# Last block pair: units in another order, the causal mask added by TensorE, and the squares for the value ranges spread over two pairs

## The chip, the cores and the metric

The kernel runs on one core of a Trainium2 chip, in one launch. TensorE (PE in the profile) multiplies matrices into PSUM, VectorE (DVE), ScalarE (ACT) and GpSimd (POOL) work on elements, and SyncE (SP) issues most of the transfers. The metric is the device time of one execution, in microseconds (us); less is better.

## The reference

One layer over 1024 rows of width 1024, in fp32. The input is normalised, scaled and shifted by terms that come from a conditioning vector, and projected to queries, keys, values and gates of two groups of eight heads of 64. One group is forgetting attention (softmax with an added term from a cumulative sum of log gates), the other stick-breaking attention. Each group's output is gated by SiLU, both are projected together, added to the input with a per-column gate, and normalised again:

```python
# forgetting attention, one block i of 128 queries against keys 0 .. 128 (i + 1)
s = einsum('bhqd,bhkd->bhqk', q, k) * HEAD_DIM ** -0.5
s = s + (f_q[..., :, None] - f_k[..., None, :])
s = where(k_pos[None, :] <= q_pos[:, None], s, -inf)
o = einsum('bhqk,bhkd->bhqd', softmax(s), v)
...
y = concat([y_fox * silu(fg), y_sb * silu(sg)]) @ w_out
x = layer_norm(ALPHA * x + gate * y) * ln_g + ln_b
```

## The kernel before

**Pairs and units.** The 16 heads are worked on as eight pairs `p` (0 to 3 stick-breaking, 4 to 7 forgetting). A unit is `(p, h, i)`: head `h` of a pair and query block `i` of 128 rows, against `i + 1` blocks of 128 keys. `order(p)` (lines 1228 to 1237) lists the 16 units of a pair; the main loop (line 1304) counts units as `k` from 0 to 127, and the last pair begins at `LAST` = 112. In the last pair the order is 7, 6 for head 0, 7, 6 for head 1, then 5, 4 twice, 3, 2 twice, 1, 0 twice.

**One unit of a forgetting pair.** `att_scores` (line 593) has PE write the scores into PSUM: two fp32r matmuls for each half of the keys (lines 606 and 607; there is one half up to 512 keys, else two). DVE adds the row `fb` of forget terms and takes the row's minimum (line 614), ACT takes the exponential with its sum (620), DVE the reciprocal (621, 622), ACT writes the high fp16 part (626) and DVE, one unit later, the low part (630). `cross` sends both through a transposing DMA on SP (567). The causal mask stands in `fb` itself: `att_causal` adds a 128x128 triangle of -1e30 to the diagonal block of the next unit's `fb` on DVE (591), in place, which works while the blocks of a head come in falling order. Five units later (`LAG_CROSSED`), when both blocks of a block pair `j` are there, `att_pv` multiplies by the values (701) and `att_sum` combines, gates and, for pairs before the last, queues a store to `y_dr` in DRAM (727, 728, 733; `send`, line 579). For the last pair the result stays on chip as `y7h` and `y7l` (738, 739). `LAST_HOMES` (538) gives each block pair of the last pair its place for the transposed parts.

**Fillers.** Between the units, PE's projection work is issued in small steps from one generator chain (`fillers`, line 1200): `gen_m(p, m)` projects q, k and the gates of pair `p`, `gen_v(g)` the values of two pairs. `FILL` says how many steps each pair takes. `beside(main, *sides)` issues one step of each side with each step of the main chain and runs the sides out at its end. The sides of the first group are `gen_gate` and `gen_ranges`. `gen_ranges` (378) loads the 12 raw value weights through the two `raw` buffers that the other weights use as well, squares and sums each on DVE (393), and three steps (`NORM_SPACE`) later comes to the next; at the end it derives a scale for each group of values, first used by `gen_v(1)`. `gen_forget` (475) is a side of a later group: it sums the log gates, and 16 steps (`FROW`) on has POOL write a triangle of ones `tri` into an `att` buffer (499, 500), which PE multiplies at once (504).

**Last pair.** Its fillers are `gen_last_g(7)` (1184): the gates, with `split_wo` beside each step, which splits one 128-row piece of the output weights into high (ACT, 1063) and low parts (half on DVE, half on POOL, 1064). The two gate accumulators use both PSUM buffers of tag `acc` and are emptied by ACT (320) and DVE (321).

**Output.** Rows come in eight tiles `t` of 128, in `OUT_ORDER`. `load_y(t)` (1077) loads the stored results of pairs 0 to 6 in two pieces and splits them on POOL (1084, 1085). `o_step` (1093) is three matmuls into an `acc` buffer (1104 to 1106), 16 such steps a tile; `o_half` (1110) applies the gate and adds the input on DVE (1123, 1124), takes statistics (1125), normalises (1132, 1136) and stores. From unit `LAST + OUT0` on, `TAIL` steps of output are issued after each unit, so the first tiles are worked on while the last pair's attention is still going; a tile's last step needs `y7h` and `y7l` of its rows.

**What sets the order.** PE's instructions stand in the order of the program (`manual_schedule`). The order on the other engines and in SP's queue is set by the framework's planner, from the same program, before the kernel runs; `after(...)` adds single constraints. Every engine and SP's queue then work through their lists in order.

Of the kernel before, what the change touches and what calls it, by code (L numbers as in the profile page):

```python
# [15 lines left out]
P = 128  # L16
SEQ = 1024
D = 1024
NB = 8
NPAIR = 8  # L20
# [11 lines left out]
def tile_hybrid_layer(  # L32
# [17 lines left out]
    nc = tc.nc  # L50
# [47 lines left out]
    GATE = 20  # L98
    NORM_SPACE = 3

# [277 lines left out]
    def gen_ranges():  # L378


        nc.gpsimd.tensor_copy(modc[:, 1, :], bss_sb[:, 1, :])
        m2 = rng[:, 0:2]
# [92 lines left out]
    def gen_forget():  # L475
# [13 lines left out]
        with after(*lows[-1:]):  # L489
# [4 lines left out]
                                     op0=ALU.add, op1=ALU.mult)  # L494
        for _ in range(FROW):
            yield
# [3 lines left out]
        nc.gpsimd.affine_select(out=tri, in_=tri, pattern=[[1, P]], base=0,  # L500
                                channel_multiplier=-1, compare_op=ALU.is_ge, fill=0.0)
        f_ps = s_tile("f_ps", 2)
        fp = f_ps[:, 0, :64]
# [33 lines left out]
    HOMES = ((1, 12), (2, 0), (1, 0), (0, 0))  # L537
    LAST_HOMES = ((1, 12), (4, 8), (2, 0), (4, 0), (1, 0), (0, 0), (0, 0), (4, 0))

# [53 lines left out]
    def att_scores(u, following):  # L593
# [10 lines left out]
        for s in halves:  # L604
            ks = slice(s * w, s * w + w)
            nc.tensor.matmul(S[:, s, :w], qst[p][h][:, qs], kst[p][h][:, ks], start=True, stop=False)  # L606
            nc.tensor.matmul(S[:, s, :w], z, klo[p][:, ks], start=False, stop=True)  # L607
        v3 = lambda a: a[:, :ke].rearrange("p (a b) -> p a b", a=ns)
        if p >= 4:
# [7 lines left out]
            pay(reduced)  # L617
            if following:
                att_causal(following)
# [467 lines left out]
    o_acc = {}  # L1087
    OUT_ORDER = (6, 7, 4, 5, 2, 3, 0, 1)

# [94 lines left out]
    def gen_last_g(p):  # L1184
# [14 lines left out]

    fillers = chain([  # L1200
        beside(chain([gen_rest(), gen_v(0, v0_w, range(4, NB)), gen_m(1, 2)]), gen_gate(), gen_ranges()),
        gen_m(2, 0), gen_m(2, 1), gen_v(1),
        beside(chain([gen_m(2, 2), gen_m(3, 0), gen_m(3, 1), gen_m(3, 2)]), gen_forget()),
# [9 lines left out]
    W0 = 100.0  # L1213
    OUT0 = 4
    TAIL = (2, 2, 2, 2, 2, 2, 4, 4, 4, 4, 8)
# [3 lines left out]
    LNLOAD = 7  # L1219
    YLOAD = (6, 9, 12, 14, 16)  # L1220
    done = [0]
# [6 lines left out]
    def order(p):  # L1228
        if p == 0:
            return [(p, h, i + d) for i in (0, 4) for h in range(2) for d in range(4)]  # L1230
        if p < FIRST_CROSSED:
            return [(p, h, i) for h in range(2) for i in range(NB)]
        if p < 4:
            return [(p, h, i + d) for h in range(2) for i in (6, 4, 2, 0) for d in range(2)]
        if p < NPAIR - 1:
            return [(p, h, i) for h in range(2) for i in reversed(range(NB))]
        return [(p, h, i + d) for i in reversed(range(0, NB, 2)) for h in range(2) for d in (1, 0)]

# [18 lines left out]
    LAST = 16 * (NPAIR - 1)  # L1257
    tail = chain([gen_out_first(6), gen_out_last(6)] + [gen_out(t) for t in OUT_ORDER[1:]])
    fill(4)
# [44 lines left out]
    for k in range(len(units) + LAG_CROSSED):  # L1304
        if k < 16 * 4:
            weights_turn(k)
            scores_turn(k)
        else:
            scores_turn(k)
            fill(want[2 * k + LEAD + 1])  # L1310
            weights_turn(k)
        send(k)
        fill(want[2 * k + LEAD + 2])
        if k >= LAST + OUT0:
            for _ in range(TAIL[min(k - LAST - OUT0, len(TAIL) - 1)]):
                next(tail, None)
        if k == LAST:
            load_y(6)
        if k == LAST + LNLOAD:
            load_ln()  # L1320
        for i, d in enumerate(YLOAD):
            if k == LAST + d:
                load_y(OUT_ORDER[i + 1])
# [64 lines left out]
```

## Time and profile before

| | |
|---|---|
| median of 3 runs | 670.23 us (669.97 to 673.47) |
| the profiled execution: its own time | 674.67 us |
| its span on the profile | 673.0 us |
| mean granted clock of TensorE | 0.976 |
| DMA, moved | 96.25 MB, mean 143 GB/s |
| all before the last pair, on the profile | 0 to 527 us |
| last pair and output, on the profile | 527 to 673 us |

All durations below are those of the profiled execution; the runs give the time. A row of a group reads: line of the kernel, engine, operation, output and input tiles, shapes, count, busy time, mean of one in ns, idle time of the engine ahead of it and who ended it. In the view of waits a row names who waited, for whom, the sum, the count and the longest. In a timeline row stand start, duration, engine, line, operation, tiles, shape, count and, in brackets, the idle time ahead and its releaser.

### The profile page before, as it was taken

How to read it: one execution, taken by the hardware profiler on the slowest of the kernel's cores; microseconds unless marked ns; L12 is line 12 of the kernel's file. 1: busy time of each engine (PE TensorE's matmuls, PEld its weight loads, DVE VectorE, ACT ScalarE, POOL GpSimd, SP SyncE). 2: the span in 40 equal slices, each digit the busy share in tenths (PEclk: the TensorE clock that was granted, in tenths of full speed). 3: DMA queues.
4: the chain of work that ended last, by engine and by line, in shares of the span. 5: the costliest groups of instructions: out<-in, count | busy, mean ns of one | idle time of the engine just before them, and what ended most of it. 6: DMA issues, size and time to landing. Idle time of an engine off the chain costs nothing. (4 is left out here: it accounts for less than half of the span.)

```text
span 673.0 us, 10856 instructions
## 1 busy us (share of the span) xinstructions
PE 634.2 (94%) x3526; PEld 532.4 (79%) x3526; DVE 518.8 (77%) x1027; ACT 398.2 (59%) x833; POOL 342.4 (51%) x429
## 2 busy tenths in 40 slices
PE   8999987999999989999999999999999859899995
PEld 4788876788899868788998888899888647688884
DVE  6787788986857887977967685876779698886756
ACT  5577354775657767677867675766659767421000
POOL 5660164965635685778566333331642376356412
PEclk9999998999999989999999999999999879799998
DMA  9983454211201164847466575865496899673301
GB/s 321 401 302 141 148 137 139 72 41 40 65 16 36 42 148 79 157 111 162 121 172 156 144 165 123 169 138 112 130 207 139 231 231 253 133 200 122 122 31 63
DMA packets 153800, 96.25 MB, mean 143 GB/s; under 512 B 118224, under 2 KB 133136, under 8 KB 153744
## 3 DMA queue, kind: packets, MB, share of 16 engines
q1 hardware_dynamic: 152160, 91.09, 53.1%
q10 hardware_dynamic: 1584, 4.47, 1.9%
q8 instruction: 28, 0.46, 0.3%
q14 instruction: 28, 0.23, 0.1%
HBM read 55.13 MB, written 7.90 MB: 94 GB/s over the span
## 5 line engine op out<-in xcount | busy, mean ns | idle before, releaser
L328 PE MATMUL m<-uh,whi 128*128 128x512 f32 x304 | 123.1, 405 | 1.6 <-DVE kl L315 1.6
L330 PE MATMUL m<-uh,wlo 128*128 128x512 f32 x304 | 120.2, 395 | 0.0
L329 PE MATMUL m<-ul,whi 128*128 128x512 f32 x304 | 120.1, 395 | 0.0
L652 POOL TENSOR_TENSOR be<-be,kp 128x127 f32<-128x127 f32 (+3 forms) x64 | 89.4, 1397 | 44.3 <-DVE kp L650 24.4
L733 POOL TENSOR_TENSOR ty<-ty,sg 64x256 f32<-64x256 f32 x64 | 47.4, 740 | 102.4 <-DVE ty L728 58.0
L646 DVE TENSOR_TENSOR_SCAN kp<-kp,floor 128x128 f32<-128x128 f32 (+3 forms) x64 | 58.5, 914 | 17.2 <-ACT kp L638 16.6
L606 PE MATMUL S<-k,q 128*128 128x512 f32 (+5 forms) x192 | 68.7, 359 | 2.1 <-DMA k<-k 2.1
L620 ACT ACTIVATE a<-a,nm 128x1024 f32<-128x1024 f32 (+3 forms) x64 | 49.7, 776 | 33.0 <-DVE nm L614 32.1
L330 PEld LDWEIGHTS m<-uh,wlo 128*128 128x128 f32 x304 | 57.4, 189 | 13.7
L328 PEld LDWEIGHTS m<-uh,whi 128*128 128x128 f32 x304 | 57.5, 189 | 12.8 <-issue 1.4
L630 DVE SCALAR_TENSOR_TENSOR home<-a,l,home 128x1024 f16<-128x1024 f32 (+3 forms) x64 | 62.7, 979 | 4.4 <-ACT home L626 3.2
L607 PE MATMUL S<-kl,qz 128*128 128x512 f32 (+5 forms) x192 | 65.9, 345 | 0.0
L329 PEld LDWEIGHTS m<-ul,whi 128*128 128x128 f32 x304 | 57.5, 189 | 9.8
L614 DVE CUSTOM_DVE_ANT_0 a<-S,fb 128x1024 f32<-128x1024 f32 (+3 forms) x64 | 48.1, 752 | 21.6 <-PE S L607 21.2
L626 ACT ACTIVATE home<-a,l 128x1024 f16<-128x1024 f32 (+3 forms) x64 | 49.2, 773 | 22.7 <-DVE l L622 11.7
L638 ACT ACTIVATE kp<-S 128x384 f32<-128x384 f32 (+4 forms) x96 | 43.7, 491 | 26.9 <-PE S L607 26.2
L701 PE MATMUL pv<-home,v_g 128*128 128x256 f16 x480 | 57.7, 269 | 1.3 <-DVE ty L728 0.7
L1104 PE MATMUL o<-woh,whi_y 128*128 128x512 f32 (+1 forms) x119 | 47.9, 403 | 11.1 <-POOL wol L1064 8.2
L701 PEld LDWEIGHTS <-v_g 128*128 128x128 f16 x480 | 44.3, 100 | 17.5 <-issue 11.8
L438 PE MATMUL v<-whi_v,uh 128*128 128x256 f32 (+1 forms) x192 | 54.7, 285 | 0.0
L440 PE MATMUL v<-wlo_v,uh 128*128 128x256 f32 (+1 forms) x192 | 54.4, 283 | 0.0
L439 PE MATMUL v<-whi_v,ul 128*128 128x256 f32 (+1 forms) x192 | 54.1, 282 | 0.0
(325 smaller groups left out, 1606.6 us busy)
## 6 DMA issues: line engine op xcount, KB each, us to landing
raw<-in_w_qkg_dram SPq DMA_DIRECT2D x38, 256.0 KB, 2.7
wss<-in_w_ss_dram SPq DMA_DIRECT2D x14, 512.0 KB, 8.4
x<-in_x_dram SPq DMA_DIRECT2D x8, 512.0 KB, 7.1
k<-k SPq DMA_DIRECT2D x32, 128.0 KB, 2.3
wg<-in_w_gate_dram SPq DMA_DIRECT2D x8, 512.0 KB, 4.9
fb<-f_dr ACTq DMA_DIRECT2D x8, 512.0 KB, 4.2
wor<-in_w_out_dram SPq DMA_DIRECT2D x8, 512.0 KB, 4.0
xr<-in_x_dram SPq DMA_DIRECT2D x8, 512.0 KB, 4.0
```

Source lines behind the costliest of these rows:

```text
L328: nc.tensor.matmul(acc, hi[:, c], u_hi[kt][:, s], start=(kt == 0), stop=False)
L329: nc.tensor.matmul(acc, hi[:, c], u_lo[kt][:, s], start=False, stop=False)
L330: nc.tensor.matmul(acc, lo[:, c], u_hi[kt][:, s], start=False, stop=(kt == NB - 1))
L438: nc.tensor.matmul(acc[:, :n], u_hi[kt][:, ts_], hi[:, s], start=(kt == 0), stop=False)
L439: nc.tensor.matmul(acc[:, :n], u_lo[kt][:, ts_], hi[:, s], start=False, stop=False)
L440: nc.tensor.matmul(acc[:, :n], u_hi[kt][:, ts_], lo[:, s], start=False, stop=(kt == NB - 1))
L606: nc.tensor.matmul(S[:, s, :w], qst[p][h][:, qs], kst[p][h][:, ks], start=True, stop=False)
L607: nc.tensor.matmul(S[:, s, :w], z, klo[p][:, ks], start=False, stop=True)
L630: lows[:] = [nc.vector.scalar_tensor_tensor(lo, ab, l, hi, op0=ALU.mult, op1=ALU.subtract)]
L646: last_dve = nc.vector.tensor_tensor_scan(rv, rv, floor[:, :ke - lo], initial=0.0, op0=ALU.mult, op1=ALU.max)
L652: nc.gpsimd.tensor_tensor(be[:, :ke - 1], be[:, :ke - 1], kp[:, 1:ke], op=ALU.mult)
L701: nc.tensor.matmul(acc[:, q0:256], vt[p][:, kb, h * P:(h + 1) * P], pt[:, 2 * kb + x_, q0:], start=(kb == 0 and x_ == 0), stop=(kb == last ...
```

## The change

The last pair's units come in the order 2, 3 for head 0, 2, 3 for head 1, then 0, 1 twice, 4, 5 twice and 6, 7 twice, and the output tiles in the order 2, 3, 0, 1, 4, 5, 6, 7; `LAST_HOMES` follows that order. As blocks no longer come in falling order, the mask of the last pair isn't added to `fb`: a third matmul, identity times triangle in fp32, adds it to the last 128 columns of the scores in PSUM, and `att_causal` is left out for the last pair. Output begins one unit later (`OUT0` 5), the first `load_y` stands at `LAST + 4` in place of `LAST`, the second at `LAST + 7` in place of `LAST + 6`.

`gen_ranges` waits for 18 steps before its first square and leaves five steps between squares; `gen_m(2, 0)` and `gen_m(2, 1)` move into the main chain that it runs beside. In `gen_forget`, `tri` is written eight steps earlier; the matmul that reads it stays where it was.

```diff
--- before.py
+++ after.py
@@ -96,7 +96,8 @@
     FLOG = 8
     FROW = 16
     GATE = 20
-    NORM_SPACE = 3
+    NORM_SPACE = 5
+    NORM_AT = 18
 
     def after(*instructions):
         stack = ExitStack()
@@ -378,6 +379,8 @@
     def gen_ranges():
 
 
+        for _ in range(NORM_AT):
+            yield
         nc.gpsimd.tensor_copy(modc[:, 1, :], bss_sb[:, 1, :])
         m2 = rng[:, 0:2]
         nc.vector.tensor_reduce(out=m2, in_=modc.rearrange("p k i -> p i k"), op=ALU.max,
@@ -492,13 +495,15 @@
         pre = ff
         nc.vector.tensor_tensor_scan(pre, flf[:, 0:64], later.rearrange("p h t -> p (h t)"), initial=0.0,
                                      op0=ALU.add, op1=ALU.mult)
-        for _ in range(FROW):
+        for _ in range(FROW - 8):
             yield
         scratch = att_tile("fscratch")
         tri, fr = scratch[:, :P], scratch[:64, P:2 * P]
         nc.gpsimd.memset(tri, 1.0)
         nc.gpsimd.affine_select(out=tri, in_=tri, pattern=[[1, P]], base=0,
                                 channel_multiplier=-1, compare_op=ALU.is_ge, fill=0.0)
+        for _ in range(8):
+            yield
         f_ps = s_tile("f_ps", 2)
         fp = f_ps[:, 0, :64]
         nc.tensor.matmul(fp, tri, lf, start=True, stop=False)
@@ -535,7 +540,7 @@
     homes, parts_at = {}, []
 
     HOMES = ((1, 12), (2, 0), (1, 0), (0, 0))
-    LAST_HOMES = ((1, 12), (4, 8), (2, 0), (4, 0), (1, 0), (0, 0), (0, 0), (4, 0))
+    LAST_HOMES = ((2, 0), (2, 4), (4, 0), (4, 8), (0, 0), (1, 0), (4, 0), (0, 0))
 
     def home(n):
 
@@ -604,7 +609,10 @@
         for s in halves:
             ks = slice(s * w, s * w + w)
             nc.tensor.matmul(S[:, s, :w], qst[p][h][:, qs], kst[p][h][:, ks], start=True, stop=False)
-            nc.tensor.matmul(S[:, s, :w], z, klo[p][:, ks], start=False, stop=True)
+            masked = p == NPAIR - 1 and s == ns - 1
+            nc.tensor.matmul(S[:, s, :w], z, klo[p][:, ks], start=False, stop=not masked)
+            if masked:
+                nc.tensor.matmul(S[:, s, w - P:w], ident, causal, start=False, stop=True)
         v3 = lambda a: a[:, :ke].rearrange("p (a b) -> p a b", a=ns)
         if p >= 4:
             a = att_tile(f"a_{p}_{h}_{i}")
@@ -615,7 +623,7 @@
                                                op0=ALU.add, op1=ALU.min, scale=-1.0, scalar=BIG,
                                                accum_out=nm)
             pay(reduced)
-            if following:
+            if following and following[0] < NPAIR - 1:
                 att_causal(following)
             nc.scalar.activation(a[:, :ke], a[:, :ke], AF.Exp, scale=-1.0, bias=nm, accum_out=l)
             nc.vector.reciprocal(l, l)
@@ -1085,7 +1093,7 @@
             nc.gpsimd.tensor_tensor(lo[:, :n * P], raw, hi.bitcast(F32)[:, :n * P], op=ALU.subtract)
 
     o_acc = {}
-    OUT_ORDER = (6, 7, 4, 5, 2, 3, 0, 1)
+    OUT_ORDER = (2, 3, 0, 1, 4, 5, 6, 7)
 
     def groups(t):
         return ((0, 512), (512, 768), (768, 1024)) if t == OUT_ORDER[-1] else ((0, 512), (512, 1024))
@@ -1198,8 +1206,9 @@
             yield
 
     fillers = chain([
-        beside(chain([gen_rest(), gen_v(0, v0_w, range(4, NB)), gen_m(1, 2)]), gen_gate(), gen_ranges()),
-        gen_m(2, 0), gen_m(2, 1), gen_v(1),
+        beside(chain([gen_rest(), gen_v(0, v0_w, range(4, NB)), gen_m(1, 2), gen_m(2, 0), gen_m(2, 1)]),
+               gen_gate(), gen_ranges()),
+        gen_v(1),
         beside(chain([gen_m(2, 2), gen_m(3, 0), gen_m(3, 1), gen_m(3, 2)]), gen_forget()),
         gen_m(4, 0), gen_m(4, 1), gen_v(2),
         gen_m(4, 2), gen_m(5, 0), gen_m(5, 1), gen_m(5, 2),
@@ -1211,13 +1220,14 @@
     LAG = 2
     LAG_CROSSED = 5
     W0 = 100.0
-    OUT0 = 4
+    OUT0 = 5
     TAIL = (2, 2, 2, 2, 2, 2, 4, 4, 4, 4, 8)
     G7 = 6
     HELD = {4: (1, 1), 5: (0, 0), 6: (1, 0), 10: (0, 1)}
     FIRST_UNITS = 5
     LNLOAD = 7
-    YLOAD = (6, 9, 12, 14, 16)
+    YFIRST = 4
+    YLOAD = (7, 9, 12, 14, 16)
     done = [0]
 
     def fill(want):
@@ -1234,7 +1244,7 @@
             return [(p, h, i + d) for h in range(2) for i in (6, 4, 2, 0) for d in range(2)]
         if p < NPAIR - 1:
             return [(p, h, i) for h in range(2) for i in reversed(range(NB))]
-        return [(p, h, i + d) for i in reversed(range(0, NB, 2)) for h in range(2) for d in (1, 0)]
+        return [(p, h, i + d) for i in (2, 0, 4, 6) for h in range(2) for d in range(2)]
 
     units = [u for p in range(NPAIR) for u in order(p)]
     k_of = {u: k for k, u in enumerate(units)}
@@ -1255,7 +1265,7 @@
     seen = set()
     ready = []
     LAST = 16 * (NPAIR - 1)
-    tail = chain([gen_out_first(6), gen_out_last(6)] + [gen_out(t) for t in OUT_ORDER[1:]])
+    tail = chain([gen_out_first(OUT_ORDER[0]), gen_out_last(OUT_ORDER[0])] + [gen_out(t) for t in OUT_ORDER[1:]])
     fill(4)
     def weights_turn(k):
         now[0] = k
@@ -1314,8 +1324,8 @@
         if k >= LAST + OUT0:
             for _ in range(TAIL[min(k - LAST - OUT0, len(TAIL) - 1)]):
                 next(tail, None)
-        if k == LAST:
-            load_y(6)
+        if k == LAST + YFIRST:
+            load_y(OUT_ORDER[0])
         if k == LAST + LNLOAD:
             load_ln()
         for i, d in enumerate(YLOAD):
```

## The prediction

> **What bounds the kernel now.** I read the page first: the busy shares, then the slices.
>
> ```profile
> span 673.0 us, 10856 instructions
> PE 634.2 (94%) x3526; PEld 532.4 (79%) x3526; DVE 518.8 (77%) x1027; ACT 398.2 (59%) x833; POOL 342.4 (51%) x429
> ...
> PE   8999987999999989999999999999999859899995
> ...
> PEclk9999998999999989999999999999999879799998
> ```
>
> PE is busy for 634.2 of 673.0 us; the 39 us in which it isn't lie in few slices: 5 and 6 (84 to 118 us), 14, and 31 to 34 (around 522 to 589 us), with a lower granted clock beside them. The next view is that of the waits, for PE alone: who released it, us in total, times, longest.
>
> ```profile
> PE o L1104 <- POOL wol L1064: 8.2, 1, 8.2
> PE v L438 <- DVE v L455: 4.1, 1, 4.1
> PE o L1104 <- DVE r L1124: 2.9, 1, 2.9
> PE f_ps L504 <- POOL fscratch L500: 2.8, 1, 2.8
> PE S L606 <- DMA k<-k: 2.1, 1, 2.1
> ...
> PE pv L712 <- DVE pt L686: 1.5, 1, 1.5
> PE gate L970 <- DVE gate L971: 1.3, 1, 1.3
> ...
> PE v L438 <- DVE kl L315: 1.0, 1, 1.0
> ```
>
> So the end is set by TensorE's own list of work, plus a few long single waits. Each part of the change sits at one of them. The busy times by stretch say which engine is full there (columns: PE, weight load, DVE, ACT, POOL, granted clock, DMA).
>
> ```profile
> 81.00:113.00 32.00, 24.60 (x147) 21.65 (x145) 23.61 (x52) 15.00 (x39) 15.98 (x23) 0.95 0.46 127
> 113.00:165.00 52.00, 50.04 (x268) 41.81 (x269) 43.34 (x73) 35.57 (x82) 40.26 (x52) 1.00 0.21 56
> 527.06:545.86 18.80, 16.74 (x80) 13.13 (x79) 12.98 (x25) 12.43 (x23) 8.58 (x9) 0.91 0.83 231
> 545.86:554.25 8.39, 0.24 (x4) 0.07 (x2) 8.39 (x13) 5.88 (x13) 8.39 (x6) 0.64 0.97 204
> 554.25:579.50 25.25, 21.65 (x113) 17.53 (x113) 22.72 (x51) 17.72 (x37) 15.24 (x16) 0.91 1.00 219
> 579.50:660.00 80.50, 80.50 (x361) 64.93 (x361) 55.64 (x109) 9.60 (x25) 34.63 (x43) 0.96 0.39 113
> ```
>
> The last pair begins at 527.06. From 545.86 to 554.25 PE stands still while DVE and POOL are full; from 579.50 on PE is full to the end. Whatever moves the first output matmul (554.28) therefore moves the end.
>
> **The long gap of the last pair.** The timeline there:
>
> ```profile
> 545.57 1.27 POOL L1085 TENSOR_TENSOR wlo_y<-yr,whi_y 128x512 fp32r<-128x512 f32 x1
> 553.46 0.67 DVE L321 SCALAR_TENSOR_TENSOR sg<-sg,m 128x512 f32<-128x512 f32 x1
> 554.28 0.77 PE L1104 MATMUL o<-woh,whi_y 128*128 128x512 f32 x1 [8.18 <-POOL wol L1064]
> 555.27 0.63 PE L1106 MATMUL o<-wol,whi_y 128*128 128x512 f32 x1
> 555.70 0.63 PE L1104 MATMUL o<-woh,whi_y 128*128 128x512 f32 x1
> ```
>
> The view names a POOL split, but the matmul's y was ready at 546.84 and it needs only the first weight tile. Both accumulators of tag `acc` still held the last gate matmuls; they are freed by line 321 on DVE, which ends at 554.13. So this wait is DVE's backlog. What fills DVE (one row for each group and shape, 500 to 600 us):
>
> ```profile
> L1064 DVE TENSOR_TENSOR wol<-wor,woh 128x512 fp32r<-128x512 f32 x8 | 9.1, 1147 | 1.0 <-ACT woh L1063 1.0
> L630 DVE SCALAR_TENSOR_TENSOR home<-a,l,home 128x1024 f16<-128x1024 f32 x3 | 6.1, 2048 | 0.0
> L591 DVE TENSOR_TENSOR fb<-fb,causal_ps 128x128 f32<-128x128 f32 x23 | 5.9, 282 | 0.1
> ...
> L614 DVE CUSTOM_DVE_ANT_0 a<-S,fb 128x1024 f32<-128x1024 f32 x3 | 3.7, 1220 | 2.5 <-PE S L607 2.5
> ...
> L630 DVE SCALAR_TENSOR_TENSOR home<-a,l,home 128x384 f16<-128x384 f32 x3 | 2.0, 675 | 0.4 <-ACT home L626 0.4
> ...
> L614 DVE CUSTOM_DVE_ANT_0 a<-S,fb 128x384 f32<-128x384 f32 x3 | 1.6, 548 | 0.0
> ```
>
> **Part 1, order of units.** A unit of i+1 blocks of 128 keys costs DVE 0.134 us a block on line 614 ((1.220-0.548)/5) and 0.275 on line 630. Ahead of line 321 stand five reductions and three low halves: before, 36 and 23 blocks (8, 7, 8, 7, 6), after, 15 and 10 (3, 4, 3, 4, 1). That is 21 x 0.134 + 13 x 0.275 = 6.4 us less, and with six mask additions (6 x 0.282 = 1.7) 8.1 us less of DVE: the whole backlog of 8.39. The wait for the second half of k (2.1 us) goes as well, since units 2 and 3 read only the first 512 keys.
>
> PE's side: two matmuls of 512 columns cover four blocks, and they follow each other at 0.23 us.
>
> ```profile
> 536.75 0.39 PE L606 MATMUL S<-k,q 128*128 128x512 f32 x1
> ...
> 537.44 0.40 PE L607 MATMUL S<-kl,qz 128*128 128x512 f32 x1
> ```
>
> That is 0.117 us a block. Before the first output matmul PE then has 21 blocks less (-2.5), five masks more (+1.2, priced below), no wait for k (-2.1) and not the clock lost behind it (18.8 x 0.09 = -1.7): it is through near 540.8 rather than 545.86. Two tanh and two of line 321 behind that free the accumulators near 543.5.
>
> What is late next is y. Rows 256 to 383 come out of pair 6's second last block pair, so `load_y(2)` stands four units later than `load_y(6)` did, behind that pair's store on SP. Here is how late such a store was:
>
> ```profile
> 542.22 0.74 POOL L733 TENSOR_TENSOR ty<-ty,sg 64x256 f32<-64x256 f32 x1 [0.30 <-POOL whi_y L1084]
> 552.89 0.58 SPq L579 DMA_DIRECT2D y_dr<-ty  x1
> ```
>
> and how long the loads of line 1081 took (min/median/max, 500 to 600 us):
>
> ```profile
> DMA to landing us min/median/max: 2.6/3.3/6.1
> ```
>
> The product was ready at 542.96 and its store was issued 9.9 us later: SP takes its list in order, and transposes that wait for line 630 stood ahead. After the change the product should be ready near 538.4 (2.1 + 1.7 + 13 x 0.117 - 3 x 0.244 = 4.6 us earlier) and those transposes wait for 3-block units; I take the store at 542, 2.4 us to land (an estimate, a little under the quickest load), 3.3 for the load, 1.3 for POOL's low half: about **549**. Ends: 543.5 if y isn't late, 561 if the store is as late as before (552.89 + 2.4 + 3.3 + 2.3). Term: 549 - 554.3 = **-5.3** (-10.8 to +6.7). Behind the waiting matmul stand all later scores on PE, and so DVE and ACT too.
>
> **Part 2, what PE has left from there.** The 21 blocks come back: +2.5. The mask is one fp32 matmul of 128 columns by 128 weights. The nearest row is line 201, eight such calls that stand as 16 instructions:
>
> ```profile
> 7.00 1.95 PE L201 MATMUL sc_all<-ident,sc 128*128 128x128 f32 x16
> ```
>
> 0.244 us a call. Eleven of the 16 masks lie behind the first output matmul: 11 x 0.244 = 2.7, and the five earlier ones are hidden under the wait. Half of that (one pass) is the lower end, nothing the lowest, if PE waits for DVE there anyway. Taken: **+5.2** (2.5 to 5.2).
>
> Behind it PE now waits 3.6 us up to 579.50 (25.25 - 21.65), 2.9 of it for line 1124. Now the large units come while output is being drained, so DVE is fuller there, but units of 7 blocks stand between the first tile's last matmul and the next accumulator. Taken: 2.8 us, so **-0.8** (-3.6 to +3).
>
> The clock: after the gap the output matmuls follow at 0.43 us (555.27, 555.70) instead of 0.23, and 0.91 is granted over the 25.25 us behind it: 2.3 us lost. The stretch with the 2.1 us wait for k has 0.91 as well, so short waits cost clock too, and I leave the ramp in the sum. The Trainium skill (TensorE: Matmul & The Clock Gate, Part 1) says that the clock halves after an idle window of about 3.4 us and is whole after as long a busy one; by that rule a gap under 3.4 us would cost no ramp, and the best rival below would come out 2.3 us lower, which the 0.91 of the first stretch speaks against.
>
> **Part 3, squares for the value ranges.**
>
> ```profile
> L393 DVE CUSTOM_DVE_ANT_0 n<-n 128x512 f32<-128x512 f32 (+1 forms) x12 | 9.6, 802 | 4.3 <-DMA n<-in_w_vf_dram 2.2 <-DMA n<-in_w_v_dram 2.1
> ```
>
> and one of them in the timeline, beside a POOL operation:
>
> ```profile
> 91.14 1.28 POOL L961 TENSOR_TENSOR wlo_gate<-gate,whi_gate 128x512 fp32r<-128x512 f32 x1
> 91.52 1.47 DVE L393 CUSTOM_DVE_ANT_0 n<-n 128x528 f32<-128x528 f32 x1 [1.05 <-DMA n<-in_w_vf_dram]
> ```
>
> All 12 lie in the first of the two stretches (81 to 113 us), take 9.6 us and hold DVE another 4.3 for their loads, 1.16 us each with both. PE's waits there (4.1, 1.5, 1.3, 1.0: 7.9 us) are all for DVE's work queued behind them. After the change they stand at steps 18, 23, ... 73, at about one us a step from 81 us on (52 steps of pair 0 in some 50 us, an estimate): three in the first stretch, nine in the second. The first stretch loses nine of 12, and I take three quarters of 7.9 as saved (-5.9). The second has 52 - 43.34 = 8.7 us of DVE free and gets 9 x 1.16 = 10.4, so 1.7 comes back: **-4.2** (-7.9 to +4). Their loads also go between the weight loads of gate 1 and of q and k 2 on SP, through the same two `raw` buffers; the weights are asked for two steps ahead only. The last range step is step 82 and the values' first use some twelve steps on, which covers it.
>
> The square at 91.52 took 1.47 us beside POOL's 1.28, against a mean of 0.80, and POOL is busy for 77% of the second stretch against 50% of the first. The Trainium skill (SBUF — State Buffer, SBUF: two separate sides) says that a DVE operation with two SBUF inputs and a GpSimd one that reads SBUF exclude each other; by that rule nine squares would pay 0.67 us in 27% more of the cases, 1.6 us, and the sum below would be 1.6 us higher.
>
> **Part 4, `tri` eight steps earlier.**
>
> ```profile
> 246.54 0.20 POOL L499 MEMSET fscratch<- 128x128 f32 x1
> 246.81 0.29 POOL L500 TENSOR_SCALAR_AFFINE_SELECT fscratch<-fscratch 128x128 f32<-128x128 f32 x1
> ```
>
> POOL writes it just in time for a PE that has waited 2.8 us; eight steps are some 8 us, so the wait goes. The price is one of six `att` buffers held for those steps; if a score tile waits for it, up to the 2.8 is lost again. Taken **-2.8** (-3.5 to 0).
>
> **Sum.** -5.3 + 5.2 - 0.8 - 4.2 - 2.8 = -7.9. The profiled execution took 674.67 us (span 673.0, 1.67 around it), so 666.8 there; the median of the runs shown is 670.23, 4.4 us below the profiled one, so **662.3** against it.
>
> **The rivals.** About 0.5% (3.4 us: below 666.8 or above 673.6) is what can be told from no change.
>
> - y late (slower). The store of pair 6's rows stays as late on SP as it is now, the first output matmul waits until 561: 670.23 - 7.9 + 12 = 674.3. It decides from 560.3 on; break-even is 556.9. For it: the 9.9 us above. Against it: what held SP was low halves of 7 and 8 blocks.
> - Squares still in the way. Half of the nine in the second stretch both wait for their load (1.1, 4.3 over four) and meet POOL (0.67): the wait counts 0.36 of the 1.16 already, so 10.4 + 4.5 x (0.74 + 0.67) = 16.7 against 8.7 free, 8.0 over instead of 1.7: 668.6, no change. For it: DVE is at 83% there. Against it: PE is the fuller engine there (50.0 of 52), so DVE may fall behind by some of it unseen.
> - The change doesn't do what it says. Only PE's order is written by hand; DVE's is the planner's, which may put line 321 behind the splits again. First output matmul at 554.3: 667.6, no change.
> - All waits go: first output matmul at 543.5 and no stall behind: 670.23 - 7.9 - 5.5 - 2.8 = 654.0.
>
> **How the numbers follow.** Forecast 0.50, all waits go 0.08 (both faster: 0.58); squares 0.14 and planner 0.14 (no change: 0.28); y late 0.14 (slower). The range, 653.5 to 673.0, takes in the best case and leaves out most of the slower one.
>
> **What would show it.** In the changed profile: the first matmul of line 1104 near 549 less the 7.0 us gained upstream, so near 542, released by y (line 1085) and not by line 321; no wait for k at the start of the last pair; PE's waits in 81 to 113 us under 3 us in all, and no new one over 2 us up to 165; no wait for fscratch; 32 mask instructions 0.12 us apart. I am wrong if the gap ahead of the first output matmul, 8.2 us by the sum (540.8 to 549), is over 12, or if PE stops for line 614 or 1124 for more than 5 us in all while the large units run.

## The result, and the profile after

The changed kernel takes 662.78 us (median of 4 runs, 661.58 to 664.71), the kernel before 670.99 in the same measurement (4 runs): ratio 0.9875, 95% interval 0.9837 to 0.9912. The forecast was 662.3. The profiled execution of the changed kernel took 664.71 us, its span is 663.0.

The sum came out; its terms did so only in part. The page of the changed kernel, its busy line and two rows of its slices:

```profile
PE 635.6 (96%) x3558; PEld 535.5 (81%) x3558; DVE 511.8 (77%) x1011; ACT 397.8 (60%) x833; POOL 344.3 (52%) x429
...
PE   8999989799999999999999999999999979999995
...
PEclk9999989899999999999999999999999989999998
```

Counted from 0, slice 14 (f_ps) is filled and the hole around slice 32 is shorter. Slice 7 is new, with the clock lower in 5 and 7. The view of waits of the changed kernel, PE alone, names what is left:

```profile
PE o L1112 <- DVE sg L322: 4.8, 2, 3.6
PE T L691 <- DVE pt L694: 3.4, 1, 3.4
PE o L1113 <- POOL y7l L747: 1.9, 1, 1.9
```

The waits for k, for the triangle and for line 455 are gone, and the one at the second tile's first matmul (2.9 us) is 0.6. The busy times of the same stretches as before, and of the last pair (same columns):

```profile
81.00:113.00 32.00, 28.80 (x182) 26.12 (x181) 26.32 (x49) 17.77 (x48) 23.16 (x31) 0.95 0.42 113
113.00:165.00 52.00, 47.71 (x232) 39.30 (x231) 41.95 (x69) 32.92 (x75) 34.28 (x43) 0.93 0.24 65
...
523.60:538.03 14.43, 14.43 (x85) 11.90 (x83) 10.15 (x26) 11.73 (x27) 7.86 (x7) 1.00 1.13 271
538.03:541.64 3.61, 0.01 (x1) 0.03 (x1) 2.59 (x10) 3.61 (x10) 2.62 (x2) 1.00 1.15 296
541.64:566.80 25.16, 22.06 (x108) 18.25 (x109) 16.71 (x43) 16.58 (x40) 18.54 (x20) 0.86 0.79 204
566.80:650.00 83.20, 82.56 (x395) 67.04 (x393) 61.84 (x105) 14.15 (x25) 37.51 (x44) 1.00 0.47 131
...
650.00:663.00 13.00, 5.37 (x46) 5.16 (x44) 7.21 (x15) 0.82 (x2) 1.84 (x4) 0.84 0.21 81
```

Up to 113 us PE does 4.2 us more than before (28.80 against 24.60); in the next stretch 2.3 us less (47.71 against 50.04), and the clock of 0.93 takes another 52 x 0.07 = 3.6. The last pair begins at 523.60, 3.5 us earlier than before. Its first output matmul comes 18.0 us behind that (541.64), where it was 27.2 (554.28 - 527.06), and from there to the end the changed kernel takes 121.4 us where the profile before had 118.7.

### The profile page after: what moved, and what is told of

The parts are those of the page before. It is cut to its first block, busy times and chain, and to the rows that moved or that the text cites. A ratio compares the mean times of both kernels' runs of the same rounds, so it can differ in the third digit from the quotient of the medians.

```text
span 663.0 us, 10902 instructions
## 1 busy us (share of the span) xinstructions
PE 635.6 (96%) x3558; PEld 535.5 (81%) x3558; DVE 511.8 (77%) x1011; ACT 397.8 (60%) x833; POOL 344.3 (52%) x429
## 5 line engine op out<-in xcount | busy, mean ns | idle before, releaser
L660 POOL TENSOR_TENSOR be<-be,kp 128x127 f32<-128x127 f32 (+3 forms) x64 | 89.9, 1405 | 44.9 <-DVE kp L658 24.2
L741 POOL TENSOR_TENSOR ty<-ty,sg 64x256 f32<-64x256 f32 x64 | 49.8, 779 | 91.6 <-DVE ty L736 56.0
L611 PE MATMUL S<-k,q 128*128 128x512 f32 (+4 forms) x192 | 68.5, 358 | 1.0 <-ACT be L648 1.0
L613 PE MATMUL S<-kl,qz 128*128 128x512 f32 (+4 forms) x192 | 65.8, 344 | 0.0
L622 DVE CUSTOM_DVE_ANT_0 a<-S,fb 128x1024 f32<-128x1024 f32 (+7 forms) x64 | 48.2, 753 | 19.7 <-PE S L613 15.8
L628 ACT ACTIVATE a<-a,nm 128x1024 f32<-128x1024 f32 (+7 forms) x64 | 49.7, 776 | 19.8 <-DVE nm L622 18.9
L638 DVE SCALAR_TENSOR_TENSOR home<-a,l,home 128x1024 f16<-128x1024 f32 (+7 forms) x64 | 58.1, 907 | 3.5 <-ACT home L634 3.3
L634 ACT ACTIVATE home<-a,l 128x1024 f16<-128x1024 f32 (+7 forms) x64 | 49.3, 773 | 16.2 <-DVE l L630 9.0
L646 ACT ACTIVATE kp<-S 128x384 f32<-128x384 f32 (+4 forms) x96 | 43.7, 491 | 23.7 <-PE S L613 21.9
L709 PE MATMUL pv<-home,v_g 128*128 128x256 f16 x480 | 56.3, 265 | 0.7 <-DVE ty L736 0.7
```

What stands on the lines that cost most here:

```text
L638: lows[:] = [nc.vector.scalar_tensor_tensor(lo, ab, l, hi, op0=ALU.mult, op1=ALU.subtract)]
L660: nc.gpsimd.tensor_tensor(be[:, :ke - 1], be[:, :ke - 1], kp[:, 1:ke], op=ALU.mult)
L709: nc.tensor.matmul(acc[:, q0:256], vt[p][:, kb, h * P:(h + 1) * P], pt[:, 2 * kb + x_, q0:], start=(kb == 0 and x_ == 0), stop=(kb == last ...
```

## The experiments

Ratios are to the kernel before, measured beside each kernel; a difference of ratios is turned into us with 671, and its uncertainty is the root of the squares of both half intervals.

### Squares as before

`NORM_SPACE` 3, no `NORM_AT`, and the two projections of pair 2 outside `beside` again.

```diff
-    NORM_SPACE = 5
-    NORM_AT = 18
+    NORM_SPACE = 3
...
```

> The changed kernel with the value ranges as before (squares from the first step on, three steps apart, the two projections of pair 2 outside). Theory of the prediction: the squares' new places are worth 4.2 us, so this is near 667.0 (662.8 + 4.2) and its PE waits in 81 to 113 us return to about 8 us. Theory from the trace of the changed kernel: 4.2 us more of PE work gets done in 81 to 113 us and as much is lost again behind the wait of 3.4 us at 127.2 us and at a granted clock of 0.93 in 113 to 165 us, so the time is that of the changed kernel, 662.8 within 1 us, with the first low part of gen_v(1) near 187.6 us in both.

Measured: 663.36 us, ratio 0.9870 (0.9849 to 0.9891). Against the changed kernel that is 0.3 us, give or take 2.9, to the wrong side: beside the changed last pair the squares' new places bring nothing that can be told. PE's waits in 81 to 113 us are back at 7.8 us, as expected, yet the last pair begins at 523.75 us, against 523.60: what the new places save up to 113 us is lost again further on. Beside the old last pair it looks different; the part on the prediction comes back to it.

### Squares on ACT, spread and at the old places

```diff
-                nc.vector.tensor_tensor_reduce(out=raw, in0=raw, in1=raw, op0=ALU.mult, op1=ALU.add, scale=1.0,
-                                               scalar=0.0, accum_out=fr[:, at:at + 1])
+                nc.scalar.activation(raw, raw, AF.Square, accum_out=fr[:, at:at + 1])
```

> The changed kernel with the 12 squares and their sums on ACT in place of DVE (one activation each). If the square of 1.69 us on DVE at 124.67 makes the wait of 3.4 us at 127.23 us and that makes the clock of 0.93 in 113 to 165 us (3.6 us), both go: 656 to 659. If DVE is late there for its other work (scans, evacuations), the wait stays and the time is 662.8 within 1 us; if ACT, which the scores wait for, becomes late in its place, it is above 663.8.

> The squares on ACT, but at their places of before (from the first step on, three apart). It tells what the spreading is worth once the squares are off DVE. Theory: with DVE free both stretches run without waits wherever the squares stand, so 658.7 within 1 us, as with the spread squares on ACT. Rival: their loads and ACT's work in 81 to 113 us hold the weights' casts up and the spreading is worth its 4 us there: 662 to 663.

Measured, spread: 658.71 us, 0.9793 (0.9769 to 0.9818), 5.5 us (give or take 3.0) faster than the changed kernel. At the old places: 665.26 us, 0.9904 (0.9872 to 0.9937), which neither theory had. So with DVE rid of the squares the old places cost 7.4 us (give or take 2.7). The timelines of that kernel, squares on ACT at the old places (ACT, DVE, PE):

```profile
99.96 0.63 ACT L393 ACTIVATE n<-n 128x512 f32<-128x512 f32 x1 [1.66 <-DMA n<-in_w_v_dram]
...
101.19 0.69 DVE L690 TENSOR_TENSOR pt<-T,pt 128x512 fp32r<-128x512 f32 x1 [2.71 <-ACT pt L689]
...
103.66 0.55 PE L437 MATMUL v<-v_home,uh 128*128 128x256 f32 x1 [4.79 <-DVE v L454]
```

A square stands at the head of ACT's list and waits 1.66 us for its own load; what PE needs stands behind it, DVE waits 2.71 us for ACT, PE 4.79 for DVE. Before the change the same stood on DVE (timeline of before):

```profile
101.33 0.69 DVE L393 CUSTOM_DVE_ANT_0 n<-n 128x512 f32<-128x512 f32 x1 [0.94 <-DMA n<-in_w_v_dram]
```

So part of PE's wait of 4.1 us there was a queue held up by a load: 0.94 us of idle DVE, and the 0.69 of the square. The rest up to line 455 at 103.98 is DVE's own work (2.0 us behind the square). The wait moves with the square to whichever engine has it. With the squares spread on DVE it is gone, though three of the 12 still wait about 1 us for their loads (86.94, 91.20 and 120.11); which of their neighbours made room was not taken apart. What then went wrong in the changed kernel, its timeline of DVE, POOL and PE shows:

```profile
124.67 1.69 DVE L396 CUSTOM_DVE_ANT_0 n<-n 128x512 f32<-128x512 f32 x1
...
126.39 0.69 DVE L694 TENSOR_TENSOR pt<-T,pt 128x512 fp32r<-128x512 f32 x1
...
123.54 2.27 POOL L660 TENSOR_TENSOR be<-be,kp 128x895 f32<-128x895 f32 x1 [3.52 <-DVE kp L658]
...
127.23 1.09 PE L691 MATMUL T<-ident,be 128*128 128x128 f32 x4 [3.38 <-DVE pt L694]
```

The square at 124.67 took 1.69 us beside POOL's 2.27, where the one at 121.73 took 0.67, and line 694, which PE waits for, stood behind it. On ACT, spread, that wait is gone, and both stretches run at the full clock (windows of that kernel):

```profile
81.00:113.00 32.00, 29.18 (x186) 25.59 (x185) 22.20 (x40) 23.26 (x66) 23.14 (x33) 1.00 0.42 113
113.00:165.00 52.00, 50.70 (x260) 41.84 (x260) 41.50 (x63) 38.90 (x92) 34.27 (x44) 1.00 0.24 71
```

### The triangle alone

The kernel before with only the four lines of `gen_forget`.

```diff
-        for _ in range(FROW):
+        for _ in range(FROW - 8):
...
+        for _ in range(8):
+            yield
         f_ps = s_tile("f_ps", 2)
```

> The kernel before with nothing but the triangle written eight steps earlier. Theory: the wait of 2.8 us for it goes and nothing is late in its place, so 2.4 to 2.8 us faster than before (ratio 0.996). Rival: as the squares seem to be worth nothing and squares and tri together 6.5 us, tri is worth about 6 (ratio 0.991). Rival: the att buffer held eight steps longer makes a score tile wait, then ratio 0.999 to 1.

Measured: 669.04 us, 0.9960 (0.9939 to 0.9981): 2.7 us, give or take 1.4. The first theory holds. Between 230 and 260 us PE waits for nothing but 1.0 us for ACT, so the held `att` buffer costs PE no wait there.

### The last pair as before, the mask alone, the order alone

Three kernels take the last pair apart: the changed kernel without its last pair's part; the kernel before with nothing but the mask's matmul; and the changed kernel with the old order of units and output rows, the mask on TensorE.

```diff
-            nc.tensor.matmul(S[:, s, :w], z, klo[p][:, ks], start=False, stop=True)
+            masked = p == NPAIR - 1 and s == ns - 1
+            nc.tensor.matmul(S[:, s, :w], z, klo[p][:, ks], start=False, stop=not masked)
+            if masked:
+                nc.tensor.matmul(S[:, s, w - P:w], ident, causal, start=False, stop=True)
...
-    OUT_ORDER = (2, 3, 0, 1, 4, 5, 6, 7)
+    OUT_ORDER = (6, 7, 4, 5, 2, 3, 0, 1)
```

The first hunk is the mask alone, the second the core of the old order.

> The changed kernel with the last pair as before (order, mask in fb on DVE, output order): before plus squares and tri. Theory of the prediction: squares and tri are worth 7.0 us and the last pair 0.9, so near 664.0, 1 us above the changed kernel. Theory from the traces: the pair begins only 3.5 us earlier, so near 667.5, and the last pair is worth 4.5 to 5; the first output matmul stands 27 us after the first scores of the pair again (18.0 in the changed kernel), released by line 322 and not by y.

> The kernel before with the last pair's mask added by TensorE alone, everything else and the order as before. If DVE's backlog sets the first output matmul, the six masks that leave DVE there (6 x 0.28 us = 1.7) bring it forward by 1.7 us, and the masks behind it cost PE 0.24 us each (10 x 0.244 = 2.4): near 671.7, 0.7 above the kernel before. If DVE isn't the limit there, all 16 cost: 674.9. If the fp32 mask matmuls hide under other waits, it is at or below 669.3.

> The changed kernel with units and output rows of the last pair in the order of before (and its places and issue times), the mask still on TensorE. It tells the order's worth from the mask's. If gains add by the medians (mask alone 3.0 us, last pair without squares and tri 0.9903 against 0.9951 with the mask alone), it is 0.9903 x 0.9951 of before, near 662.2 against 671.99 here, about 1 us below the changed kernel: the order is worth nothing. If they add by stretches of the profiles (pair and output take 142.6 us with the mask alone, 139.4 in the changed kernel), it is 3.2 us above the changed kernel, 666 to 667.

Measured: without the last pair's part 665.23 us, 0.9903 (0.9884 to 0.9922); the mask alone 669.03, 0.9951 (0.9933 to 0.9970); the old order with the mask 666.81, 0.9923 (0.9899 to 0.9947). So beside the triangle and the moved squares the whole part of the last pair is worth 1.9 us (give or take 2.8) and the order in it 3.2 (give or take 3.0). The mask does not add: alone it brought 3.3 us (give or take 1.3), the third of its expectations; beside the other two parts it cost 1.3 (0.9923 against 0.9903, give or take 2.1), which can't be told from nothing. The stretches of the profiles, in us; the first three rows have the same code in the last pair:

| kernel | the pair starts at | to the first output matmul | from there to the end | both |
|---|---|---|---|---|
| before | 527.06 | 27.2 | 118.7 | 145.9 |
| triangle alone | 522.61 | 26.1 | 116.4 | 142.5 |
| last pair as before | 522.80 | 26.7 | 114.1 | 140.8 |
| mask alone | 524.31 | 27.3 | 115.3 | 142.6 |
| old order, with the mask | 522.59 | 24.2 | 118.3 | 142.6 |
| squares as before | 523.75 | 17.2 | 121.2 | 138.4 |
| the changed kernel | 523.60 | 18.0 | 121.4 | 139.4 |

The same code took 140.8 to 145.9 us in three profiles, so one profile of each kernel can't tell a difference of that size in the sum. The way to the first output matmul scatters less (26.1 to 27.2), and there the order shows: 24.2 to 18.0. The mask alone leaves it where it was (27.3). The waits at the second tile's first matmul, in the kernel before (first row), with all but the last pair's part (second), with the mask alone (third):

```profile
PE o L1104 <- DVE r L1124: 2.9, 1, 2.9
```

```profile
PE o L1109 <- DVE r L1129: 1.7, 1, 1.7
```

```profile
PE o L1107 <- DVE r L1127: 0.8, 1, 0.8
```

Before, the clock behind that wait was 0.70 for 10.5 us (579.5 to 590.0), 3.2 us lost; behind the waits of 1.7 and 0.8 it was 1.00. The profiles of before and of the mask alone differ behind the first output matmul (118.7 and 115.3), as this loss would have it. Whether the 3.3 us of the medians are this wait and its clock is not shown: the profile of before lies 3.7 us above the median of its kernel (674.67 against 670.99), and the kernel with the triangle alone, which has its mask on DVE too, waited 1.7 us there with the clock at 1.00. What the mask alone brought stays open.

The second kernel also corrects the account of the end. The sums of the windows from the first output matmul to the end, of before and of the kernel without the last pair's part (the first figure is the length, the second PE's busy time):

```profile
sum 118.72, PE 107.49 PEld 87.56 DVE 85.50 ACT 28.14 POOL 51.70; mean PE 35.83 PEld 29.19 DVE 28.50 ACT 9.38 POOL 17.23
```

```profile
sum 114.10, PE 104.78 PEld 85.80 DVE 83.61 ACT 28.20 POOL 51.88; mean PE 34.93 PEld 28.60 DVE 27.87 ACT 9.40 POOL 17.29
```

The old order took 114.1 us in the profile in which the clock held behind the second tile's wait; the profile before had 4.6 us more. The changed kernel takes 121.4 us with PE busy for 110.0 (22.06 + 82.56 + 5.37 in its windows above): 7.3 us longer, 5.2 of it busy. Busy time is not work alone: a matmul of line 1114 lasted 0.40 us at 542.18 and 0.63 at 544.79, where the clock was low. By count, 19 blocks and 10 masks more stand behind the first output matmul; a mask took 0.22 us (from 523.95 to the next matmul at 524.17), so the work is 19 x 0.117 + 10 x 0.22 = 4.4 us.

### The mask in one pass

```diff
-                nc.tensor.matmul(S[:, s, w - P:w], ident, causal, start=False, stop=True)
+                high = lambda a: a.bitcast(BF16).rearrange("p (c two) -> p c two", two=2)[:, :, 1]
+                nc.tensor.matmul(S[:, s, w - P:w], high(ident), high(causal), start=False, stop=True)
```

> The changed kernel with the mask's matmul in bf16 (the upper halves of identity and triangle, which are exact for 1 and 0 and near -1e30) in place of fp32, so one pass for two. Theory: the 11 masks behind the first output matmul cost PE their full 0.24 us, so half of it goes: 11 x 0.12 = 1.3 us, 661.5 against 662.8 (ratio 0.9855). Rival: hidden by the waits there, no change within 0.5 us.

Measured: 663.90 us, 0.9895 (0.9863 to 0.9927): no gain. The mask stands as one instruction instead of two, but the planner placed DVE's work differently: the first output matmul came 15.2 us after the pair's start (537.52 against 522.36), and the one for the second accumulator waited 4.71 us, until 20.8 (543.17), against 20.2 in the changed kernel (543.77). The second accumulator sets the pace there, so the price of a pass isn't told by this run.

### TensorE kept busy in its wait

```diff
+        if pr == 0 and h == 0 and t == OUT_ORDER[0]:
+            warm = pv_tile("warm", 1)
+            for _ in range(12):
+                nc.tensor.matmul(warm, qst[NPAIR - 1][0][:, :P], kst[NPAIR - 1][0][:, :512], start=True, stop=True)
```

> The changed kernel with 12 matmuls of 512 columns more on TensorE ahead of the first output matmul, into a PSUM buffer that nobody reads. They fill 12 x 0.23 = 2.8 us of its wait of 3.6 us. Theory: what a wait of over 2 us costs beyond itself is the clock of 0.65 and 0.50 in the 8 us behind (3.4 us lost); with TensorE at work the clock stays whole and the kernel is faster for more work: near 659.5, ratio 0.982. Rival: the clock in those 8 us is due to something else (the 1.2 us wait that follows, the kind of work): no change, ratio 0.9875. Rival: the planner's order behind them moves the waits elsewhere: slower than 663.5.

Measured: 662.90 us, 0.9871 (0.9843 to 0.9899), no change. The clock did what the theory said. The 8 us behind the first output matmul, in the changed kernel:

```profile
541.64:545.64 4.00, 2.80 (x9) 2.04 (x9) 3.94 (x8) 3.88 (x10) 2.94 (x3) 0.65 1.01 337
545.64:549.64 4.00, 4.00 (x16) 3.18 (x16) 1.96 (x9) 2.17 (x6) 4.00 (x5) 0.50 1.21 274
```

and with the 12 matmuls ahead of it, where 40 instead of 25 matmuls get done:

```profile
539.81:543.81 4.00, 2.79 (x16) 2.11 (x17) 3.94 (x8) 3.93 (x11) 2.94 (x3) 1.00 0.90 323
543.81:547.81 4.00, 4.00 (x24) 3.46 (x23) 3.41 (x14) 2.92 (x10) 4.00 (x5) 1.00 1.27 267
```

But then PE waits at the second tile's first matmul, in this kernel's timeline:

```profile
563.94 0.50 PE L1116 MATMUL o<-woh,whi_y 128*128 128x512 f32 x1 [3.52 <-DVE r L1136]
```

where the changed kernel waited 1.90 and 0.64 us. DVE is full in the first of the windows above and POOL in the second (3.94 and 4.00 of 4.00 us). I read this so: up to the emptying of the first tile it is not PE that sets the pace, and what PE wins there, it waits off.

### The splits of the output weights out of the way

In the 3.61 us before the first output matmul of the changed kernel ACT is full (3.61) and DVE isn't (2.59). Its timeline of ACT shows the tanh of line 321 behind a pair of casts and an exponential:

```profile
538.76 1.14 ACT L1071 CAST woh<-wor 128x512 fp32r<-128x512 f32 x2
539.80 0.40 ACT L628 ACTIVATE a<-a,nm 128x128 f32<-128x128 f32 x1
...
540.20 0.58 ACT L321 ACTIVATE sg<-m 128x512 f32<-128x512 f32 x1
```

Two kernels, both with the squares on ACT, put the splits of pieces 5 to 7 behind the emptying of the gate accumulators: all at once, or one after each of the first three pairs of output steps. The diff shows part of the second; the casts also stand `after` the emptying there.

```diff
+                if h and LATE_WO + pr < NB:
+                    split_wo(LATE_WO + pr)
...
-                for ch in (1, 0):
-                    evac_m(p, 2, ch, accs[ch])
-            split_wo(n)
+                emptied[:] = [evac_m(p, 2, ch, accs[ch]) for ch in (1, 0)]
+            if n < LATE_WO:
+                split_wo(n)
```

> The kernel with the squares on ACT, and with the splits of the last three pieces of the output weights behind the emptying of the gate accumulators. Theory: what the first output matmul waits for is tanh on ACT (line 321 of the changed kernel), which stands behind casts of line 1071 (1.13 us a pair), and line 322 behind it; with one pair of casts fewer ahead of the first tanh and two fewer ahead of the second the two waits of 3.2 and 1.1 us fall to under 2.5 in all, and the clock of 0.87 in the 25 us behind rises: 655 to 657 against 658.7. Rival: ACT is full there in any case, or the pieces come late for their output steps: 658.7 or more.

> As the kernel with squares on ACT and the last three pieces of the output weights split behind the gates, but the three splits one output step pair apart in place of all at once. There two splits took 1.74 us each on DVE beside POOL's two (0.68 alone), and PE waited 3.0 us for line 736 behind them at 538.18. Theory: that wait goes or falls under 1 us, and the clock of 0.57 behind it: 3 us faster, 653 against 656. Rival: the pieces come late for the output steps that need them or the next wait (line 1132, 2.7 us) grows by as much: 656 within 1 us.

> The fastest kernel so far (squares on ACT, the last three splits behind the gates and spread; 654.9, ratio 0.9739) with ten matmuls of 512 columns more on TensorE in its wait of 2.66 us ahead of the first output matmul, into a buffer that nobody reads (10 x 0.23 = 2.3 us). There the wait was followed by a clock of 0.50 and 0.71 in the next 8 us (3.2 us lost), and PE waited only 2.1 us more to the end. Theory: the clock stays whole, and PE gains the 3.2 us less what it then waits at y7 (1 to 2 us): 652 to 654, ratio 0.970 to 0.972. Rival: DVE, ACT and POOL set the pace up to the first tile's last step, and the waits there grow by all that was won, as they did in the changed kernel: 655, ratio 0.974.

Measured: all at once 655.98 us, 0.9767 (0.9736 to 0.9799), 1.7 us (give or take 2.7) below the squares on ACT alone; spread 654.90, 0.9739 (0.9709 to 0.9768), 3.6 us (give or take 2.6) below them. At once, the wait at the output fell to 2.21 and 0.59 us, but a new one stood behind the splits (timeline of DVE, POOL and PE of that kernel):

```profile
533.91 3.48 DVE L1072 TENSOR_TENSOR wol<-wor,woh 128x512 fp32r<-128x512 f32 x2
...
533.88 2.96 POOL L1072 TENSOR_TENSOR wol<-wor,woh 128x512 fp32r<-128x512 f32 x2 [2.84 <-ACT woh L1071]
...
538.18 1.43 PE L709 MATMUL pv<-home,v_g 128*128 128x256 f16 x8 [2.98 <-DVE ty L736]
```

Spread, that one is gone, and PE's waits from 529 us to the end are 2.7 (line 323), 1.0, 0.9 and 0.2 us. Ten more matmuls in the 2.7 us gave 654.75, 0.9728 (0.9705 to 0.9752), no change that can be told: the clock held there too (1.00 over the 8 us behind), and waits of 2.6 us (transposed parts) and 2.2 (second tile) took their place. This last and the spread version are the fastest, about 1.4% below the changed kernel (0.9739 and 0.9728 against 0.9875).

## Why the prediction came out

**The long gap: right in its cause, wrong in what came next.** The gap was DVE's backlog ahead of line 321, and the reordering removed it: from the pair's start to the first output matmul it is 24.2 us with the old order and the mask, 18.0 with the new order. That this matmul stands where it was foreseen (541.64 against "near 542") is luck: the pair began 3.5 us earlier instead of 7.0, and the way took 18.0 us instead of 21.9 (549 - 527.06). It is released by line 322, not by y (timeline of the changed kernel, PE and DVE):

```profile
537.33 0.36 PE L611 MATMUL S<-k,q 128*128 128x256 f32 x1
...
541.64 0.47 PE L1112 MATMUL o<-woh,whi_y 128*128 128x512 f32 x1 [3.61 <-DVE sg L322]
...
540.81 0.69 DVE L322 SCALAR_TENSOR_TENSOR sg<-sg,m 128x512 f32<-128x512 f32 x1
...
543.04 0.68 DVE L322 SCALAR_TENSOR_TENSOR sg<-sg,m 128x512 f32<-128x512 f32 x1
```

So the step "what is late next is y" failed. I had read the split at 545.57 as the one that the first output matmul needs. The first piece of y, pairs 0 to 3, is loaded and split long before in both kernels, and these rows of before were there to be read (timeline, SP's queue and POOL):

```profile
494.58 0.38 SPq L1081 DMA_DIRECT2D yr<-y_dr  x1
...
507.72 2.13 POOL L1085 TENSOR_TENSOR wlo_y<-yr,whi_y 128x512 fp32r<-128x512 f32 x1
```

The second piece, which does hang on pair 6's store, is needed only from the output step of pair 4 on. So this term was -9.2 us (27.2 to 18.0), not -5.3, and the rival "y late" had no ground. Within the term the sizes held nearly: PE was through 14.4 us after the pair's start (foreseen 540.8 - 527.06 = 13.7). The prediction counted five units ahead of it, but output begins one unit later, and six stand there, the last with 256 keys at 537.33. The first accumulator was free at 17.9 us and the second at 20.1 (foreseen 16.4 for both); ACT, not DVE, was then the full engine.

**What PE has left: near in work, wrong in waits.** Predicted were +5.2 us for 21 blocks and 11 masks. With six units ahead it is 19 and 10, and the work came to 4.4 us. The step that failed is "stalls behind it, -0.8": against the kernel without the last pair's part, waits and clock came out at +2.9 (7.3 - 4.4), against the profile that the term was read from at -1.7 (118.7 to 121.4, less 4.4). That profile had lost 3.2 us of clock behind the wait for line 1124. As the same code took 114.1 to 118.7 us in three profiles, the sign of this term stays open.

**Squares: the price was read wrongly.** I priced DVE's time (nine squares against 8.7 us free). Seven squares stayed in the first stretch, not three, and DVE's time was not all of the price: at the old places a load held a list up, at the new ones a square took 1.69 us beside POOL, with 3.4 us of waiting behind it. The clock behind that took 3.6 us in the profile of the changed kernel; in the four other kernels with the squares at these places on DVE it was 0.97 there, 1.6 us, behind the same wait. That is the rival "squares still in the way", in one place instead of four or five. The 1.6 us that I gave to the rule of the Trainium skill (SBUF — State Buffer, SBUF: two separate sides) were a mean; the trace agrees with the rule (1.69 against 0.67), but the cost came at the one square that PE stood behind.

**Triangle: right**, -2.7 measured for -2.8.

**The sum.** Four of the kernels have the triangle, with and without each of the other two parts. Their ratios to the kernel before:

| | last pair as before | last pair changed |
|---|---|---|
| squares as before | 0.9960 | 0.9870 |
| squares moved | 0.9903 | 0.9875 |

Beside the old last pair the squares' new places bring 3.8 us (give or take 1.9), beside the new one they cost 0.3 (2.9). The last pair brings 6.0 us (2.0) without the moved squares and 1.9 (2.8) with them. Together the two parts bring 4.2 us (give or take 3.5) less than each alone would add up to, so neither has one worth. In the order triangle, squares, last pair the steps are 2.7, 3.8 and 1.9 us, where the prediction had 2.8, 4.2 and 0.9; with the last pair before the squares they are 2.7, 6.0 and -0.3. Why the two overlap is not shown. In the profiles the last pair starts no earlier with the moved squares (522.80 against 522.61, 523.60 against 523.75), so the 3.8 us of the medians can't be seen there, in one execution of each.

That the forecast came within 0.5 us is therefore in part luck: in the profiles a gap term 3.9 us too small stands against a last pair that began 3.5 us earlier instead of 7.0.

**The signs I had named.** No wait for k, none for the triangle, 3.2 us of PE waits in 81 to 113 us (under 3 foreseen), 0.6 for line 1132: as said or nearly. The release of the first output matmul by y was wrong, and so was "no new one over 2 us up to 165" (3.4 at 127.23).

## What to carry to other kernels

An instruction whose operand comes by DMA costs an in-order engine its wait on top of its duration: whoever stands behind it pays, on whichever engine it is put, so look for a place where nobody who is needed stands behind. When a long wait goes, read the next one from the rows of the very tile that the waiting instruction names, and check which of several pieces it is. Compare stretches with more than one kernel that has the old code there, or the clock of one execution is booked on the change. And take parts out alone and together: removed one at a time from the changed kernel, the squares looked worthless here.

## What the runs showed of the hardware

The clock behind a wait of PE, over 14 profiles from 60 us on: each of the 19 waits of over 3 us was followed by a mean granted clock of 0.50 to 0.65 over the next 4 us; of the 19 waits of 2.0 to 3.0 us 11 were followed by 0.50 to 0.75, 8 by the whole clock, the longest of these 2.79 us; of the 23 of 1.4 to 1.95 us two were followed by less than the whole clock (0.75 and 0.81). The low values gather at 0.50 and 0.57, that is, half the clock for all of the 4 us or for 3.4 of them. So a wait over 3 us takes about 1.7 to 3.4 us of clock beyond itself. The Trainium skill (TensorE: Matmul & The Clock Gate, Part 1) has the clock halve after about 3.4 us idle; here 2.06 us (0.67) could be enough, and the measurement decides.

Twelve matmuls that nobody reads kept the clock whole through a wait of 3.6 us (1.00 in the 8 us behind, where it had been 0.65 and 0.50), ten through one of 2.7. That is shown; that it pays is not, in either kernel where it was tried.
